# Recurrent branch of a hybrid encoder block: outputs of two row halves in one PSUM bank and one chain, the far score block issued with the step ahead of it, first scores one k tile later

## The chip, the cores and the metric

The kernel runs on one core of one Trainium2 chip. The time is device microseconds from launch to end, the median of several executions; the kernel before has 1391.43 us as the median of 3 runs (1390.93 to 1392.01). One more execution was profiled: it took 1390.61 us, of which the program's own instructions span 1388.9 us (1.7 us lie around them).

## The reference

One block over 256 rows of width 2048, in fp32: an RMSNorm, one wide projection, two branches side by side, a gated merge, an output projection, a second RMSNorm and a squared-ReLU MLP of width 8192, and a final norm. The change lies in the recurrent branch (HGRN2): 8 heads of 128 by 128, in chunks of 64 rows.

```python
f = sigmoid(hf); g = lb + (1 - lb) * f; log_g = log(g); kk = 1 - g
q = silu(hq) * 128 ** -0.5
# per head, chunk after chunk, b = cumsum(log_g) in the chunk:
o_inter = (q * exp(b)) @ S
scores  = sum_k q[t,k] * exp(b[t,k] - b[s,k]) * kk[s,k]     # s <= t
o       = o_inter + scores @ v
S       = exp(b_last)[:, None] * S + (kk * exp(b_last - b)).T @ v
y_a     = rms_norm(o, hg_norm_w) * silu(hg)
```

The other branch is chunked attention (16 heads of 64) with a relative bias, and comes behind the recurrent one in the kernel.

## The kernel before, in words

Every large product takes its operands as two fp32r parts, high and low. A weight tile of 128x1024 comes in by a DMA on SyncE's queue (`raw`), ScalarE (ACT) casts it into `wh` (line 91) and VectorE (DVE) subtracts to get `wl` (line 92); `wh` and `wl` have four buffers each, so the cast for a tile waits until TensorE (PE) has used up the tile four before it. `gemm_t` (lines 163 to 185) gives feature-major results, per k tile two matmuls of 512 columns with `wh` and two of 256 with `wl`; `gemm` (line 154) gives row-major ones, per k tile six matmuls of 512 columns. Both write `acc` tiles of two banks from the pool `ps_acc`, which has two buffers.

The recurrent branch has no stage of its own on PE. Its small fp32 matmuls are laid between the k tiles of the big products by a list of steps, `behind`: `later` appends steps with a number each, and `tick` (lines 144 to 149), called per k tile with 1 in `gemm_t` and 2 in `gemm`, counts the front step's number down and issues it when it reaches zero. Steps are issued in the order of the list. The scheduler then keeps the order of issue on each engine, except that what is issued at high priority (the weight splits, line 125; results, line 187; the last split of the outputs, line 491) goes ahead as soon as its inputs are expected.

The eight heads are four pairs (0 to 3). `scores` (line 515) appends for a pair the eight steps that `hgrn_scores` (line 357) returns at line 457: the first step (tiles `ps_10`, `ps_11`, one per head, then the factors of level 2), then factors and levels in turn. A level (line 406) multiplies for each head into a bank `ps` of pool `ps_sm` (tag "sm", two banks), and three predicated copies of DVE per head (line 421) merge it into the tile `sd` of a pair: `ps_20`, `ps_21` are level 2 of heads 0 and 1, likewise `ps_80` and `ps_320`. `level128` (line 442) makes the far block between the two row halves: two matmuls into `ps_128`, which ACT copies to `so`.

`hgrn_out` (line 461) makes the outputs of a pair. `outputs(m)` for row half m: `po` (`sd` times the values `v`, and for m = 1 also `so` times `v` of half 0) into a bank of `ps_sm`; ACT squares it (line 477), DVE sums the squares (478) and scales the sum (line 97), GpSimd (POOL) raises it to -0.5 (line 98), DVE multiplies `po` by that and the gate `gw` into `o` (483). `finish(m)` transposes the two heads' `o` into a bank `tpo` of pool `ps_tp` (tag "tp", two banks), and a split on ACT and DVE makes `act_ya`. `group` (line 533) appends the outputs of two pairs, and returns their finishing steps.

The calls at lines 545 to 561 set the order: the scores of pair 0 beside the products `hi` and `hg` of heads 0 to 3, those of pair 1 beside `hg`, `hf`, `hq`, the outputs of pairs 0 and 1 beside `hf` and `hq` of pair 3, and so on; the outputs of pairs 2 and 3 beside the products `aq`, behind which attention begins. A product is named by its column block in the traces: `acc_hi`, `acc_hq`, `acc_aq`, `acc_ak`. `aq0T` is the copy of the first `aq` product (lines 189 and 190).

Of the kernel before, what the change touches and what calls it, by code (L numbers as in the profile page):

```python
# [8 lines left out]
F32 = mybir.dt.float32  # L9
# [3 lines left out]
ALU = mybir.AluOpType  # L13
AX = mybir.AxisListType
PSUM = bass.MemoryType.PSUM

P = 128
T = 256
NM = T // P
# [7 lines left out]
DK = 128  # L27
# [23 lines left out]
def tile_hybrid_block(  # L51
# [5 lines left out]
    nc = tc.nc  # L57
# [14 lines left out]
    ident = const.tile([P, P], F32, name="ident")  # L72
# [17 lines left out]
    def split(hi, lo, src, copy=None):  # L90
        casts[:] = [(copy or nc.scalar.copy)(hi, src)]  # L91
        return nc.vector.tensor_tensor(lo, src, hi.bitcast(F32), op=ALU.subtract)  # L92

    def rsqrt(dst, ssq, n, width):

        ms = small.tile([P, width], F32, name="ms", tag=f"ms{width}")
        nc.vector.tensor_scalar(ms, ssq, 1.0 / n, EPS, op0=ALU.mult, op1=ALU.add)  # L97
        nc.gpsimd.tensor_tensor(dst, ms, mhalf[:, :width], op=ALU.pow)  # L98

# [51 lines left out]
    def later(*steps):  # L151
        behind.extend([n, f] for n, f in steps)
# [41 lines left out]
    hp = hpool_cm.__enter__()  # L194
# [164 lines left out]
    def hgrn_scores(n, made):  # L359

        kk, b, q = made["kk"], made["b"], made["q"]
        sd = hp.tile([P, 2, NM, P], F32, name=f"sd{n}", tag="sd", bufs=2)
        so = hp.tile([P, 2, P], F32, name=f"so{n}", tag="so", bufs=2)
# [77 lines left out]

        def level128():
            kc, ql = held["128"]
            ps = ps_sm.tile([P, 2, P], F32, name=f"ps{n}_128", tag="sm")
            for h in range(2):
                nc.tensor.matmul(ps[:, h, :], kc[:, h].rearrange("p v b -> p (v b)"),
                                 ql[:, h].rearrange("p v b -> p (v b)"), start=True, stop=True)
            nc.scalar.copy(so, ps)

        f = [lambda i=i, B=B: factors(i, B) for i, B in enumerate(LEVELS)]  # L450
        l = [lambda i=i, B=B: level(i, B) for i, B in enumerate(LEVELS)]
# [2 lines left out]
            diagonal()  # L454
            f[0]()

        return (sd, so), [first, f[1], l[0], f[2], l[1], factors128, l[2], level128]

    ya = []

    def hgrn_out(g, h0, sc, vs, gws):
        sd, so = sc
        n = f"{g}{h0}"
        hi, lo = ya[g][:, :, 0, :], ya[g][:, :, 1, :]
        os = []

        def outputs(m):
            po = ps_sm.tile([P, 2, DK], F32, name=f"po{n}{m}", tag="sm")
            for h in range(2):
                c = slice((h0 + h) * DK, (h0 + h + 1) * DK)  # L470
                if m:
                    nc.tensor.matmul(po[:, h, :], so[:, h, :], vs[0][:, c], start=True, stop=False)
                nc.tensor.matmul(po[:, h, :], sd[:, h, m, :], vs[m][:, c], start=m == 0, stop=True)
            o = hp.tile([P, 2, DK], F32, name=f"o{n}{m}", tag="o", bufs=4)
            sq = hp.tile([P, 2, DK], F32, name=f"osq{n}{m}", tag="osq", bufs=1)
            s2 = small.tile([P, 2], F32, name=f"os{n}{m}", tag="os")
            nc.scalar.activation(sq, po, AF.Square)
            nc.vector.tensor_reduce(s2, sq, axis=AX.X, op=ALU.add)
            ro = small.tile([P, 2], F32, name=f"ro{n}{m}", tag="ro")
            rsqrt(ro, s2, DK, 2)  # L480
            for h in range(2):
                c = slice((h0 + h) * DK, (h0 + h + 1) * DK)
                nc.vector.scalar_tensor_tensor(o[:, h, :], po[:, h, :], ro[:, h:h + 1], gws[m][:, c],
                                               op0=ALU.mult, op1=ALU.mult)
            os.append(o)

        def finish(m):
            tp = ps_tp.tile([P, 2, P], F32, name=f"tpo{n}{m}", tag="tp")
            for h in range(2):
                nc.tensor.transpose(tp[:, h, :], os[m][:, h, :], ident)  # L490
            with tc.high_priority(offset=2000):
                split(hi[:, h0:h0 + 2, m * P:(m + 1) * P], lo[:, h0:h0 + 2, m * P:(m + 1) * P], tp)

        return [lambda m=m: outputs(m) for m in range(NM)], [lambda m=m: finish(m) for m in range(NM)]

    def fq(u):
        if u == 0:
            f, z = f0, z0
        elif u == 1:
            f, z = f1, z1  # L500
        else:
            f, z = h2(f"f{u}"), h2(f"zq{u}")
            add_parts(f, gemm_t(xT, w_in_t, C_HF + u * T, KD, f"hf{u}"))
            add_parts(z, gemm_t(xT, w_in_t, C_HQ + u * T, KD, f"hq{u}"))
        made = {}

        def decay():
            made["g"], made["kk"], made["b"] = hf_pair(u, f)

        def query():  # L510
            made["q"] = hq_pair(u, z, made["g"])

        return made, decay, query

    def scores(n, made, gap, first=None, between=()):

        sc = []
        steps = []
# [8 lines left out]
        todo = [(gap if i or first is None else first, lambda i=i: one(i)) for i in range(8)]  # L527
        for at, f in between:
            todo.insert(at, (gap, f))
        later(*todo)  # L530
        return sc

    def group(g, s0, s1, vs, gws, gap, gap2):
        parts = {}

        def outputs(h0, sc, m):
            if not m:
                parts[h0] = hgrn_out(g, h0, sc, vs, gws)
            parts[h0][0][m]()

        later(*[(gap, lambda h0=h0, sc=sc, m=m: outputs(h0, sc, m)) for h0, sc in ((0, s0), (2, s1)) for m in range(NM)])
        return [(gap2, lambda h0=h0, m=m: parts[h0][1][m]()) for h0 in (0, 2) for m in range(NM)]
# [538 lines left out]
    for qd in range(NQ):  # L1081
# [70 lines left out]
        for n0 in (0, 2):  # L1152
# [3 lines left out]
                              start=0, tail=last and n0 == 2))  # L1156
# [47 lines left out]
```

## Time and profile before

| what | before |
|---|---|
| median of 3 runs | 1391.43 us |
| profiled execution | 1390.61 us |
| its span | 1388.9 us |
| PE busy | 1377.7 us, 99% |
| DVE busy | 1139.5 us, 82% |
| ACT busy | 925.6 us, 67% |
| POOL busy | 144.4 us, 10% |
| granted PE clock | 1.00 |
| recurrent steps on PE | 60.9 to 236 us |

A row of a group or of the timeline names the line, engine and operation, the tile written and the tiles read, and the shape; buffer numbers are left out. A small fp32 matmul stands as two records. A matmul's recorded length (0.39 us for 512 columns) overlaps the next one's; what it takes of PE is the distance from its start to the next start.

### The profile page before, as it was taken

Reading aid. Unit: us, or ns where it says so; the run is one execution under the profiler, and the core shown is the slowest. Engines: PE = TensorE matmul, PEld = TensorE weight load, DVE = VectorE, ACT = ScalarE, POOL = GpSimd, SP = SyncE. Lnnn points to the kernel's source line nnn. Section 1 sums busy time; section 2 is a strip of 40 time slices with the busy share of each in tenths; the row PEclk is TensorE's granted clock in tenths of the full one; section 3 lists DMA queues with packets and bytes.
Section 4 is the critical chain, followed back from the end, with each engine's and each line's share of the span. In section 5 each row is a group of like instructions: output and inputs, shape, how many; then the busy total and the mean of one; then the engine's idle time right before and its main releaser. Section 6 shows DMA issues by size and latency. Waiting matters only on the chain.

```text
span 1388.9 us, 18633 instructions
## 1 busy us (share of the span) xinstructions
PE 1377.7 (99%) x6550; PEld 1144.0 (82%) x6550; DVE 1139.5 (82%) x1429; ACT 925.6 (67%) x1193; POOL 144.4 (10%) x231
## 2 busy tenths in 40 slices
PE   9999999999999999999999999999999999999997
PEld 8889888878778888888888888888888888888886
DVE  7897997976878785697998977879877897878885
ACT  7774765665676664446777766678666876668864
POOL 2000001100100000001211001100011001110200
PEclk9999999999999999999999999999999999999999
DMA  9654445785679896558989789988899888998892
GB/s 339 226 175 158 153 166 178 224 280 167 161 213 279 265 268 222 191 171 272 287 224 309 246 257 299 259 255 252 249 291 301 249 236 251 277 299 260 259 283 100
DMA packets 124078, 331.62 MB, mean 239 GB/s; under 512 B 11072, under 2 KB 11840, under 8 KB 123600
## 3 DMA queue, kind: packets, MB, share of 16 engines
q1 hardware_dynamic: 103696, 265.59, 54.2%
q0 software_dynamic: 19568, 64.04, 23.5%
q8 instruction: 51, 0.84, 0.2%
q10 hardware_dynamic: 720, 0.81, 0.2%
q14 instruction: 43, 0.35, 0.1%
HBM read 271.67 MB, written 10.49 MB: 203 GB/s over the span
## 4 chain that ended last, share of the span: by engine, by line
PE 96%; DVE 2%; ACT 1%; issue 0%; DMA 0%; POOL 0%; SPq 0%; POOLq 0%; DVEq 0%; ACTq 0%
PE acc_ak L177 2%; PE acc_hf L177 2%; PE acc_aq L177 2%; PE acc_hq L177 2%; PE ps L414 1%; PE acc_ak L182 1%; PE tp_u L108 1%; PE acc_hg L136 1%; PE acc_hg L135 1%; PE acc_bb L135 1%; PE acc_bb L136 1%; PE acc_ba L135 1%; PE acc_ba L137 1%; PE acc_hg L137 1%; PE acc_ba L136 1%; PE acc_bb L137 1%
## 5 line engine op out<-in xcount | busy, mean ns | idle before, releaser
L177 PE MATMUL acc_aq<-act_x,wh_aq 128*128 128x512 f32 x128 | 42.4, 407 | 0.0
L177 PE MATMUL acc_hf<-act_x,wh_hf 128*128 128x512 f32 x128 | 41.4, 405 | 0.0
L177 PE MATMUL acc_hq<-act_x,wh_hq 128*128 128x512 f32 x128 | 40.7, 399 | 0.0
L177 PE MATMUL acc_ak<-act_x,wh_ak 128*128 128x512 f32 x128 | 40.1, 396 | 0.1
L91 ACT CAST wh_bb<-raw_bb 128x1024 fp32r<-128x1024 f32 x16 | 16.9, 1054 | 23.3 <-PE acc_ba L137 17.7
L91 ACT CAST wh_aq<-raw_aq 128x1024 fp32r<-128x1024 f32 x16 | 16.8, 1051 | 22.5 <-PE acc_hg L137 8.7
L92 DVE TENSOR_TENSOR wl_bb<-raw_bb,wh_bb 128x1024 fp32r<-128x1024 f32 x16 | 19.6, 1224 | 14.8 <-ACT wh_bb L91 14.8
L91 ACT CAST wh_ba<-raw_ba 128x1024 fp32r<-128x1024 f32 x16 | 16.8, 1053 | 21.0 <-PE acc_bb L137 13.8
L92 DVE TENSOR_TENSOR wl_ba<-raw_ba,wh_ba 128x1024 fp32r<-128x1024 f32 x16 | 19.6, 1224 | 12.6 <-ACT wh_ba L91 12.6
L92 DVE TENSOR_TENSOR wl_aq<-raw_aq,wh_aq 128x1024 fp32r<-128x1024 f32 x16 | 19.6, 1223 | 11.1 <-ACT wh_aq L91 11.1
L182 PEld LDWEIGHTS acc_hq<-act_x,wl_hq 128*128 128x128 f32 x128 | 23.4, 188 | 6.0 <-DVE wl_hq L92 0.8
L182 PEld LDWEIGHTS acc_ak<-act_x,wl_ak 128*128 128x128 f32 x128 | 23.5, 188 | 5.6 <-issue 0.3
L182 PEld LDWEIGHTS acc_hf<-act_x,wl_hf 128*128 128x128 f32 x128 | 23.6, 189 | 5.3
L182 PEld LDWEIGHTS acc_aq<-act_x,wl_aq 128*128 128x128 f32 x128 | 23.5, 189 | 4.8
L182 PE MATMUL acc_aq<-act_x,wl_aq 128*128 128x256 f32 x128 | 25.8, 285 | 0.0
L135 PE MATMUL acc_hi<-wh_hi,act_x 128*128 128x512 f32 x64 | 25.8, 403 | 0.0
L92 DVE TENSOR_TENSOR act_u<-tp_u,act_u 128x512 fp32r<-128x512 f32 x32 | 21.9, 686 | 4.7 <-ACT act_u L91 4.2
L98 POOL TENSOR_TENSOR ro<-ms,mhalf 128x2 f32<-128x2 f32 x8 | 5.9, 738 | 190.3 <-DVE ms L97 190.3
L135 PE MATMUL acc_hg<-wh_hg,act_x 128*128 128x512 f32 x64 | 25.7, 401 | 0.0
L135 PE MATMUL acc_bb<-wh_bb,act_yb 128*128 128x512 f32 x64 | 25.2, 393 | 0.0
L136 PE MATMUL acc_hi<-wl_hi,act_x 128*128 128x512 f32 x64 | 25.1, 392 | 0.0
L182 PE MATMUL acc_hq<-act_x,wl_hq 128*128 128x256 f32 x128 | 24.7, 279 | 0.4 <-DVE wl_hq L92 0.4
(1928 smaller groups left out, 5250.6 us busy)
## 6 DMA issues: line engine op xcount, KB each, us to landing
raw_hi<-in_w_in_n_dram SPq DMA_DIRECT2D x16, 512.0 KB, 4.1
raw_hg<-in_w_in_n_dram SPq DMA_DIRECT2D x16, 512.0 KB, 3.6
raw_aq<-in_w_in_t_dram SPq DMA_DIRECT2D x16, 512.0 KB, 3.9
raw_ak<-in_w_in_t_dram SPq DMA_DIRECT2D x16, 512.0 KB, 3.8
raw_ba<-in_w_branch_a_dram SPq DMA_DIRECT2D x16, 512.0 KB, 4.4
raw_bb<-in_w_branch_b_dram SPq DMA_DIRECT2D x16, 512.0 KB, 4.4
raw_hf<-in_w_in_t_dram SPq DMA_DIRECT2D x12, 512.0 KB, 3.6
raw_hq<-in_w_in_t_dram SPq DMA_DIRECT2D x12, 512.0 KB, 4.5
```

The costliest lines, as they stand in the source:

```text
L91: casts[:] = [(copy or nc.scalar.copy)(hi, src)]
L92: return nc.vector.tensor_tensor(lo, src, hi.bitcast(F32), op=ALU.subtract)
L98: nc.gpsimd.tensor_tensor(dst, ms, mhalf[:, :width], op=ALU.pow)
L108: nc.tensor.transpose(tp[:, j, :], src[:, j * P:(j + 1) * P], ident)
L135: nc.tensor.matmul(acc, hi, wh, start=first, stop=False, skip_group_check=True)
L136: nc.tensor.matmul(acc, hi, wl, start=False, stop=False, skip_group_check=True)
L137: nc.tensor.matmul(acc, lo, wh, start=False, stop=last, skip_group_check=True)
L177: nc.tensor.matmul(acc[:, cb, :], wh[:, cb * P:(cb + 1) * P], r.rearrange("p u t -> p (u t)"), start=kt == 0, stop=last)
L182: nc.tensor.matmul(acc[:, cb, 0:T], wl[:, cb * P:(cb + 1) * P], r[:, 0, :], start=False, stop=False)
L414: nc.tensor.matmul(ps[:, m, :], klf[:, a * P:(a + 1) * P], qrf[:, a * 192:(a + 1) * 192], start=True, stop=True)
```

## The change

Three things change.

1. `level128` is no longer a step of its own: it is issued right behind the last level, in one step, and its bank comes from `ps_tp` and no longer from `ps_sm`. A pair has 7 score steps and no longer 8.
2. `outputs` makes both row halves at once: one bank `po` of 128 x (2 x 2 x 128), one square, one sum, one scaling (in place), one power, and four products into one `o`. `finish` transposes all four blocks into one bank and makes one split of 128x512. The number of a step of outputs goes from 4 to 6 for pairs 0 and 1 and from 2 to 3 for pairs 2 and 3, that of a finishing step from 3 and 2 to 6.
3. The number of pair 0's first step goes from 13 to 15, which is one k tile of `gemm`.

```diff
-    def rsqrt(dst, ssq, n, width):
+    def rsqrt(dst, ssq, n, width, ms=None):
-        ms = small.tile([P, width], F32, name="ms", tag=f"ms{width}")
+        if ms is None:
+            ms = small.tile([P, width], F32, name="ms", tag=f"ms{width}")
...
         def level128():
-            ps = ps_sm.tile([P, 2, P], F32, name=f"ps{n}_128", tag="sm")
+            ps = ps_tp.tile([P, 2, P], F32, name=f"ps{n}_128", tag="tp")
...
-        return (sd, so), [first, f[1], l[0], f[2], l[1], factors128, l[2], level128]
+        def final():
+            l[2]()
+            level128()
+        return (sd, so), [first, f[1], l[0], f[2], l[1], factors128, final]
...
-        def outputs(m):
-            po = ps_sm.tile([P, 2, DK], F32, name=f"po{n}{m}", tag="sm")
+        def outputs():
+            po = ps_sm.tile([P, NM, 2, DK], F32, name=f"po{n}", tag="sm")
+            for m in range(NM):
+                for h in range(2):
+                    c = slice((h0 + h) * DK, (h0 + h + 1) * DK)
+                    if m:
+                        nc.tensor.matmul(po[:, m, h, :], so[:, h, :], vs[0][:, c], start=True, stop=False)
+                    nc.tensor.matmul(po[:, m, h, :], sd[:, h, m, :], vs[m][:, c], start=m == 0, stop=True)
...
+            nc.vector.tensor_reduce(s2, sq.rearrange("p m h d -> p (m h) d"), axis=AX.X, op=ALU.add)
+            rsqrt(ro, s2, DK, NM * 2, s2)
...
-        def finish(m):
-            tp = ps_tp.tile([P, 2, P], F32, name=f"tpo{n}{m}", tag="tp")
+        def finish():
+            tp = ps_tp.tile([P, 2, T], F32, name=f"tpo{n}", tag="tp")
+            for m in range(NM):
+                for h in range(2):
+                    nc.tensor.transpose(tp[:, h, m * P:(m + 1) * P], os[0][:, m, h, :], ident)
...
-    s0 = scores(0, a0[0], 5, 13, ((5, a1[1]), (8, a1[2])))
+    s0 = scores(0, a0[0], 5, 15, ((5, a1[1]), (8, a1[2])))
-    turns0 = group(0, s0, s1, vs0, gws0, 4, 3)
+    turns0 = group(0, s0, s1, vs0, gws0, 6, 6)
-    later(*group(1, s2, s3, vs1, gws1, 2, 2))
+    later(*group(1, s2, s3, vs1, gws1, 3, 6))
```

The program's order shows three places. The first is PE at pair 0's first scores, beside the product `hi`. Before, `ps_10` stood ahead of the first matmul of k tile 6 and `ps_11` one matmul later:

```order
L137 MATMUL acc_hi_650<-wh_hi_4_688,act_x_108 128x512
L370 MATMUL ps_10_713<-q_646,kk_636 128x192 x2
L135 MATMUL acc_hi_650<-wh_hi_6_706,act_x_108 128x512
L370 MATMUL ps_11_718<-q_646,kk_636 128x192 x2
L136 MATMUL acc_hi_650<-wl_hi_6_707,act_x_108 128x512
L137 MATMUL acc_hi_650<-wh_hi_6_706,act_x_108 128x512
```

After the change both stand together behind the six matmuls of that k tile (line numbers of the change are one higher here):

```order
L138 MATMUL acc_hi_650<-wh_hi_6_706,act_x_108 128x512
L136 MATMUL acc_hi_650<-wh_hi_6_706,act_x_108 128x512
L137 MATMUL acc_hi_650<-wl_hi_6_707,act_x_108 128x512
L138 MATMUL acc_hi_650<-wh_hi_6_706,act_x_108 128x512
L371 MATMUL ps_10_719<-q_646,kk_636 128x192 x2
L371 MATMUL ps_11_724<-q_646,kk_636 128x192 x2
L136 MATMUL acc_hi_650<-wh_hi_6_706,act_x_108 128x512
```

So `ps_10` moved back by six matmuls of 512 columns and `ps_11` by five.

The second place is DVE at the outputs of pairs 0 and 1. Before, the sum (478), its scaling (97) and the products that wait for POOL (483) stood right behind one another, with a weight split between two such chains:

```order
L478 TENSOR_REDUCE os_1416<-osq_1415 128x2
L97 TENSOR_SCALAR ms<-os_1416 128x2
L483 SCALAR_TENSOR_TENSOR o_1414<-po_1411,ro_1419,gw_1067 128x128 x2
L92 TENSOR_TENSOR wl_hq_4_1550<-raw_hq_4_1548,wh_hq_4_1549 128x1024
L478 TENSOR_REDUCE os_1454<-osq_1453 128x2
L97 TENSOR_SCALAR ms<-os_1454 128x2
L483 SCALAR_TENSOR_TENSOR o_1452<-po_1447,ro_1457,gw_1071 128x128 x2
```

Now the chain of pair 0 stands among the factors of pair 2 (`b`, `el_2`, `er_2`, `q`):

```order
L322 SCALAR_TENSOR_TENSOR b_1480<-reset,lg_1478 128x512
L484 TENSOR_REDUCE os_1394<-osq_1393 128x4
L382 TENSOR_TENSOR el_2_1624<-b_1480 128x512
L98 TENSOR_SCALAR os_1394<-os_1394 128x4
L387 TENSOR_TENSOR er_2_1627<-b_1480 128x64x6
L490 SCALAR_TENSOR_TENSOR o_1392<-po_1385,ro_1397,gw_1071 128x128 x2
L490 SCALAR_TENSOR_TENSOR o_1392<-po_1385,ro_1397,gw_1075 128x128 x2
L92 TENSOR_TENSOR wl_hq_0_1524<-raw_hq_0_1522,wh_hq_0_1523 128x1024
L333 SCALAR_TENSOR_TENSOR q_1503<-zq_1080,sq_1501 128x4x128
```

Pair 2's work on DVE moved ahead of the outputs, and one chain stands where two were.

The third place is PE at the first scores of pair 2. Before, they stood behind k tile 2 of the second `hi` product:

```order
L135 MATMUL acc_hi_1644<-wh_hi_2_1669,act_x_107 128x512
L136 MATMUL acc_hi_1644<-wl_hi_2_1670,act_x_107 128x512
L137 MATMUL acc_hi_1644<-wh_hi_2_1669,act_x_107 128x512
L370 MATMUL ps_10_1699<-q_1590,kk_1562 128x192 x2
L370 MATMUL ps_11_1704<-q_1590,kk_1562 128x192 x2
```

Now they stand in the last quarter of the product ahead of it, `hq` of pair 3:

```order
L178 MATMUL acc_hq_1521<-act_x_109,wh_hq_8_1574 128x512 x2
L183 MATMUL acc_hq_1521<-act_x_109,wl_hq_8_1575 128x256 x2
L178 MATMUL acc_hq_1521<-act_x_110,wh_hq_12_1603 128x512 x2
L183 MATMUL acc_hq_1521<-act_x_110,wl_hq_12_1604 128x256 x2
L371 MATMUL ps_10_1614<-q_1503,kk_1475 128x192 x2
L371 MATMUL ps_11_1619<-q_1503,kk_1475 128x192 x2
```

Between the two positions lie the last three k tiles of `hq` (six matmuls of 512 columns, six of 256) and the first four of `hi` (24 of 512 columns): that far did the scores of pair 2 move forward. Pair 1's first scores moved forward in the same way by four k tiles of `gemm_t`, and each later level with them.

More of the change, by code (lines that the diff above doesn't have):

```diff
@@ L487, in finish @@
[L487 to L490 removed]
+        def outputs():
[6 more added lines that the diff above has]
+                    nc.tensor.matmul(po[:, m, h, :], sd[:, h, m, :], vs[m][:, c], start=m == 0, stop=True)
+            o = hp.tile([P, NM, 2, DK], F32, name=f"o{n}", tag="o", bufs=2)
+            sq = hp.tile([P, NM, 2, DK], F32, name=f"osq{n}", tag="osq", bufs=1)
+            s2 = small.tile([P, NM * 2], F32, name=f"os{n}", tag="os")
+            nc.scalar.activation(sq, po, AF.Square)
+            nc.vector.tensor_reduce(s2, sq.rearrange("p m h d -> p (m h) d"), axis=AX.X, op=ALU.add)
+            ro = small.tile([P, NM * 2], F32, name=f"ro{n}", tag="ro")
+            rsqrt(ro, s2, DK, NM * 2, s2)
+            for m in range(NM):
+                for h in range(2):
+                    c = slice((h0 + h) * DK, (h0 + h + 1) * DK)
+                    nc.vector.scalar_tensor_tensor(o[:, m, h, :], po[:, m, h, :], ro[:, 2 * m + h:2 * m + h + 1], gws[m][:, c],
+                                                   op0=ALU.mult, op1=ALU.mult)
+            os.append(o)
@@ L491, in finish @@
+        def finish():
+            tp = ps_tp.tile([P, 2, T], F32, name=f"tpo{n}", tag="tp")
+            for m in range(NM):
+                for h in range(2):
+                    nc.tensor.transpose(tp[:, h, m * P:(m + 1) * P], os[0][:, m, h, :], ident)
             with tc.high_priority(offset=2000):
-                split(hi[:, h0:h0 + 2, m * P:(m + 1) * P], lo[:, h0:h0 + 2, m * P:(m + 1) * P], tp)
-        return [lambda m=m: outputs(m) for m in range(NM)], [lambda m=m: finish(m) for m in range(NM)]
+                split(hi[:, h0:h0 + 2, :], lo[:, h0:h0 + 2, :], tp)
@@ L496, in fq @@
+        return outputs, finish
     def fq(u):
@@ L525, in one @@
             steps[i]()
-        todo = [(gap if i or first is None else first, lambda i=i: one(i)) for i in range(8)]
+        todo = [(gap if i or first is None else first, lambda i=i: one(i)) for i in range(7)]
         for at, f in between:
@@ L534, in group, with outputs @@
         parts = {}
[L536 to L542, printed above, removed]
+        def outputs(h0, sc):
+            parts[h0] = hgrn_out(g, h0, sc, vs, gws)
+            parts[h0][0]()
+        later(*[(gap, lambda h0=h0, sc=sc: outputs(h0, sc)) for h0, sc in ((0, s0), (2, s1))])
+        return [(gap2, lambda h0=h0: parts[h0][1]()) for h0 in (0, 2)]
     ya += [new_act(f"ya{g}") for g in range(2)]
```

15 lines of the change are left out of this document (removed).

## The prediction

> **What bounds the kernel now.** I read the page's busy times first, then busy time by stretches.
>
> ```profile
> span 1388.9 us, 18633 instructions
> PE 1377.7 (99%) x6550; PEld 1144.0 (82%) x6550; DVE 1139.5 (82%) x1429; ACT 925.6 (67%) x1193; POOL 144.4 (10%) x231
> ...
> 60.00:100.00 40.00, 39.72 (x183) 33.16 (x182) 39.37 (x91) 28.80 (x40) 0.00 (x0) 1.00 0.50 172
> 130.00:160.00 30.00, 29.93 (x180) 26.15 (x179) 24.34 (x46) 22.41 (x31) 3.15 (x4) 1.00 0.45 153
> 160.00:190.00 30.00, 30.00 (x145) 25.72 (x144) 30.00 (x74) 21.27 (x31) 0.00 (x0) 1.00 0.45 153
> 400.00:1380.00 980.00, 980.00 (x4421) 810.97 (x4421) 804.29 (x780) 669.29 (x805) 108.75 (x136) 1.00 0.85 253
> ```
>
> PE bounds it everywhere: from 400 us on it is busy in all of 980 us, at full clock, and the recurrent steps (61 to 236 us) run beside it. The change leaves PE the same matmuls, so it can win only time that PE loses waiting. Recorded busy time hides most of that, since a matmul's recorded length overlaps the next one; I measure it from start to start. DVE is the second engine: 24.34 of 30 us busy beside the outputs of pairs 0 and 1, but all 30.00 of 30 beside the scores of pair 2, and 39.37 of 40 beside those of pair 0.
>
> **Fewer, larger groups on PE: nothing.** The change merges 12 groups of small matmuls into others (4 far blocks, 4 outputs, 4 transposes). Does leaving the large product and coming back cost something?
>
> ```profile
> 70.97 1.46 PE L414 MATMUL ps<-qr,kl 128*128 128x192 f32 x8
> 72.13 0.53 PE L135 MATMUL acc_hi<-wh_hi,act_x 128*128 128x512 f32 x1
> 72.50 0.40 PE L136 MATMUL acc_hi<-wl_hi,act_x 128*128 128x512 f32 x1
> ```
>
> Eight records of 0.33 us ending 1.46 us after their first start are (1.46 - 0.33) / 7 = 0.161 apart. A 512-column matmul takes 0.227 (rows 60.20 and 60.42 below stand 0.22 apart, and longer undisturbed stretches give 0.227). From 70.97 to 72.50 are 1.53 us; 8 x 0.161 + 0.227 = 1.52. The 0.37 us behind the group only pays back its last record's early handover. The upper bound would be that 0.14 us each, 12 x 0.14 = 1.7 us; the sum above excludes nearly all of it, and I take 0.
>
> **First scores one k tile later: gain 0.8 us.**
>
> ```profile
> 60.20 0.39 PE L136 MATMUL acc_hi<-wl_hi,act_x 128*128 128x512 f32 x1
> 60.42 0.39 PE L137 MATMUL acc_hi<-wh_hi,act_x 128*128 128x512 f32 x1
> 60.90 0.92 PE L370 MATMUL ps<-q,kk 128*128 128x192 f32 x4
> 61.52 0.53 PE L135 MATMUL acc_hi<-wh_hi,act_x 128*128 128x512 f32 x1
> 62.24 0.92 PE L370 MATMUL ps<-q,kk 128*128 128x192 f32 x4 [0.18 <-DVE q L335]
> 62.86 0.52 PE L136 MATMUL acc_hi<-wl_hi,act_x 128*128 128x512 f32 x1
> 63.22 0.39 PE L137 MATMUL acc_hi<-wh_hi,act_x 128*128 128x512 f32 x1
> ...
> 60.56 0.28 DVE L335 TENSOR_TENSOR q<-q,f 128x128 f32<-128x128 f32 x1
> 61.90 0.29 DVE L335 TENSOR_TENSOR q<-q,f 128x128 f32<-128x128 f32 x1
> ```
>
> From 60.42 to 63.22 are 2.80 us, with work for 3 x 0.227 + 8 x 0.161 = 1.97: PE lost 0.83 us waiting for `q` of each head, the second written at 62.19. Six large matmuls later PE comes to `ps_10` at 60.42 + 7 x 0.227 = 62.01 and to `ps_11` at 62.66, behind both. What is late next: `ps_20` then also comes 1.36 - 0.83 = 0.5 us later than now, and DVE has its factors ready before that; cost 0, and if that cover went, at most the 0.5 us.
>
> **Waits for a bank: gains 0.28, 0.55 and 0.37 us.**
>
> ```profile
> 155.45 0.62 PE L177 MATMUL acc_hq<-act_x,wh_hq 128*128 128x512 f32 x2
> 156.14 0.44 PE L490 MATMUL tpo<-ident,o 128*128 128x128 f32 x2
> 156.34 0.48 PE L135 MATMUL acc_hi<-wh_hi,act_x 128*128 128x512 f32 x1
> 156.65 0.40 PE L136 MATMUL acc_hi<-wl_hi,act_x 128*128 128x512 f32 x1
> ...
> 155.66 0.43 DVE L92 TENSOR_TENSOR act_ya<-tpo,act_ya 128x256 fp32r<-128x256 f32 x1
> ...
> 227.82 0.39 PE L182 MATMUL acc_aq<-act_x,wl_aq 128*128 128x256 f32 x2
> 228.53 0.46 PE L472 MATMUL po<-v,so 128*128 128x128 f32 x2 [0.32 <-DVE o L483]
> 228.82 0.39 PE L473 MATMUL po<-v,sd 128*128 128x128 f32 x2
> ...
> 227.77 0.61 DVE L483 SCALAR_TENSOR_TENSOR o<-po,ro,gw 128x128 f32<-128x128 f32 x2 [0.87 <-POOL ro L98]
> ...
> 237.59 0.63 PE L177 MATMUL acc_aq<-act_x,wh_aq 128*128 128x512 f32 x2
> 238.30 0.73 PE L177 MATMUL acc_ak<-act_x,wh_ak 128*128 128x512 f32 x2
> 238.87 0.28 PE L182 MATMUL acc_ak<-act_x,wl_ak 128*128 128x256 f32 x1
> ...
> 236.16 0.37 ACT L91 CAST act_ya<-tpo 128x256 fp32r<-128x256 f32 x1
> 236.42 0.59 ACT L189 COPY aq0T<-acc_aq 128x512 f32<-128x512 f32 x1
> 237.57 0.68 DVE L190 TENSOR_TENSOR aq0T<-acc_aq,aq0T 128x512 f32<-128x512 f32 x1
> ```
>
> The third transpose waits until DVE has emptied the first one's bank (155.66 + 0.43 = 156.09): 155.45 to 156.65 is 1.20 us for three large matmuls and two records of about 0.12, that is 0.92; lost 0.28. The fourth `po` waits for the bank that `o` frees at 228.38: 0.48 us before it (two 256-column matmuls at 0.116) and 0.07 within, 0.55. The first `acc_ak` waits for the bank of the first `aq` product, which ACT copies only behind the last `act_ya` cast (236.16) and DVE adds until 238.25: 237.59 to 238.87 is 1.28 us for four matmuls, 0.91; lost 0.37. With one `po` and one `tpo` per pair, two banks serve two pairs without reuse; in the order the last transposes now stand behind the first k tile of the second `aq` product, fifteen k tiles (15 x 2 x (0.227 + 0.116) = 10.3 us) ahead of the first `acc_ak`, and `aq0T` can follow about 2 us behind them. All three waits go. Together with the first scores: 0.83 + 0.28 + 0.55 + 0.37 = 2.0 us.
>
> **What the chains cost now: 0.4 us.** A chain now is square, sum, scaling, power, four products. DVE pays POOL's latency four times, not eight:
>
> ```profile
> 223.59 0.17 DVE L97 TENSOR_SCALAR ms<-os 128x2 f32<-128x2 f32 x1
> 223.91 0.69 POOL L98 TENSOR_TENSOR ro<-ms,mhalf 128x2 f32<-128x2 f32 x1 [71.24 <-DVE ms L97]
> 224.63 0.35 DVE L483 SCALAR_TENSOR_TENSOR o<-po,ro,gw 128x128 f32<-128x128 f32 x1 [0.87 <-POOL ro L98]
> ...
> L1131 POOL TENSOR_TENSOR rstd<-rstd,mhalf x2: 553/566/578, 1377.1 to 1382.3; 128x1 f32<-128x1 f32 x2
> ```
>
> A power takes 0.57 us for one column and 0.69 for two; four are by that line 0.69 + 2 x 0.12 = 0.94 (bounds 0.69 and 1.38). The products then start 1.04 + 0.25 = 1.3 us behind the scaling. Queued behind them on DVE stand weight splits of 1.23 us, which PE needs 4 to 5 us later; they cover it.
>
> ```profile
> 235.00 1.05 ACT L91 CAST wh_ak<-raw_ak 128x1024 fp32r<-128x1024 f32 x1
> ...
> 236.09 1.23 DVE L92 TENSOR_TENSOR wl_ak<-raw_ak,wh_ak 128x1024 fp32r<-128x1024 f32 x1 [0.43 <-ACT wh_ak L91]
> ```
>
> The tight place is the last pair's transpose: in the order its fourth product stands behind `wl_aq_8`, whose cast can start only when PE frees a buffer, five k tiles (5 x 0.69 = 3.4 us) ahead of that transpose; cast 1.05, split 1.23 and product 0.35 are 2.63 before any handover or any other work of DVE. So 0 to 1.2 us (one split more in front) for this pair, the same at most for the others; I take 0.4 for all, near the lower end because the three others have 2 us to spare.
>
> [...]
>
> **Score banks: 0.3 us.** The scores of pair 2 come to PE six 512-column matmuls, six of 256 (0.116) and 24 of 512 earlier, 30 x 0.227 + 6 x 0.116 = 7.5 us. They use the two banks that `po` held, and each next level waits for DVE's copies out of the last one. That work leaves the full stretch (30.00 of 30) for the one with 5.7 us free, and DVE itself saves up to four POOL waits of 0.87, 3.5 us. Where a weight split stands before the copies, they are late by 1.23 us. Bounds 0 and four levels x 1.23 = 4.9; no `ps` wait of this kind shows even in the full stretch, so I take 0.3.
>
> **Attention's start: 0, bounds -0.9 and +0.9 us.** Its first scores move five k tiles ahead of their place, because `aq0T` is early. PE loses 0.9 us in the 150 us behind its start:
>
> ```profile
> 250.00:400.00 150.00, 149.08 (x801) 117.67 (x800) 121.31 (x208) 96.41 (x168) 16.03 (x34) 1.00 0.69 205
> ```
>
> It can go or double.
>
> **Sum.** -2.0 + 0.4 + 0.3 + 0 = -1.3 us. The profiled execution took 1390.6 us, 1388.9 of span and 1.7 around it; it becomes 1389.3. The median of the runs is 0.8 us above the profiled one: 1391.4 - 1.3 = **1390.1 us**, 0.1% faster.
>
> **Rivals.**
> - *More comes back* (12%): no chain is late, the score banks cost nothing, and attention's 0.9 us go too: -2.9 us, 1388.5, just over 0.2%. For it speaks DVE's saving; against it that some of attention's waits are for ACT's own copies, which the change leaves.
> - *Attention takes it back* (12%): its first scores, now ahead of DVE's last weight splits, wait 0.7 us more at two places: -1.3 + 1.4 us, about 1391.5, no change.
> - *Score banks bind* (14%), slower: pair 2's levels each wait for copies behind a split, four times 1.23 us, 4.9 - 2.0 + 0.4 = +3.3, 1394.7. It decides from the point where DVE comes more than about 1 us behind its present distance to PE at pair 2's second level; a POOL power near 1.4 us twice in front of that would do half of it. The 30.00 of 30 us speak for it, the 5.7 us free before against it.
> - *The change does not do what it says*: the order shows the moves, and the banks' owners are fixed by the tiles; no chance of its own.
>
> **How the numbers follow.** My forecast, -2.0 to -0.3 us, has 62%. Faster by over 0.2% (2.8 us, about what a measurement of this kernel can tell from no change) is the first rival, 12%; slower by over 0.2% the third, 14%; within is the forecast and the second rival, 74%. The range runs from 1388.4 to 1393.4: the first rival's price less the runs' scatter of 0.5 below it would be 1388.0, which I cut a little; above it takes in half of the third rival.
>
> **What would show it.** Right: from 60 to 250 us no gap at `q`, `tpo`, `po` and `acc_ak`; the `hi` and `hq` products of pair 2 start at the times above less 0.8 to 1.5 us; attention's first scores about 6 us earlier; nothing else moves behind 400 us but by a constant of 1 to 2 us. Wrong: PE rows of `ps` with DVE `sd` as releaser between 150 and 176 us; a POOL power over 1.2 us; `tpo` waiting for `o` by more than 0.5 us; or a loss from 250 to 320 us above 1 us.

## The result, and the profile after

The changed kernel takes 1389.14 us (median of 21 runs, 1388.22 to 1390.24) against 1391.62 us for the kernel before (21 runs): 2.5 us less, a ratio of 0.9984 with a 95% interval of 0.9978 to 0.9990, which is 1.4 to 3.1 us. The forecast was 1.3 us less. Four executions of the whole study, which took 300 us more or longer, are left out of all medians and intervals. The profiled execution took 1389.94 us, above its own median, while that of before lay below its own, so the two spans differ by only 0.8 us. To compare the kernels themselves I take two matmuls that both have: the last of k tile 5 of the product `hi` (in the prediction's row 60.42 for before) and the first `wh_ga0r` matmul behind a `pa`, near 390 us. In every kernel of this study the second is the 1777th record behind the first. I call the time between them the **distance**. It is read from one profiled execution of each kernel. How well it repeats shows in its last 700 records, in attention: they take 131.25 to 131.50 us in the eleven kernels that have them in the order of the changed kernel, and 131.19 to 131.27 us in the three that have them in the order of before. A difference of 0.3 us says little by itself. First two rows of the page after, then the matmul starts that bound the distance, of after:

```profile
span 1388.1 us, 18593 instructions
...
PE 1376.7 (99%) x6550; PEld 1143.5 (82%) x6550; DVE 1137.7 (82%) x1417; ACT 922.7 (66%) x1185; POOL 143.4 (10%) x227
```

```profile
60.72 0.39 PE L138 MATMUL acc_hi<-wh_hi,act_x 128*128 128x512 f32 x1
...
390.94 0.50 PE L136 MATMUL acc_ga0c<-wh_ga0r,act_x 128*128 128x512 f32 x1
```

and the second of them before:

```profile
393.11 0.50 PE L135 MATMUL acc_ga0c<-wh_ga0r,act_x 128*128 128x512 f32 x1
```

Before it is 393.11 - 60.42 = 332.69 us, after 390.94 - 60.72 = 330.22: 2.47 us less, the difference of the medians. The rest of the two spans (0.3 us more ahead of 60 us, 1.4 us more behind 393) is scatter of single executions: over the fourteen profiles the first of the two matmuls starts at 60.4 to 61.9 us, and the last matmul ends 987.8 to 989.2 us behind the second. Busy time by stretches after, with the columns as in the prediction's table (the stretch and its length; busy us and number of instructions of PE, PE's weight loads, DVE, ACT and POOL; granted clock, DMA share, GB/s):

```profile
60.00:100.00 40.00, 40.00 (x189) 34.03 (x188) 39.49 (x90) 29.13 (x41) 0.00 (x0) 1.00 0.53 182
130.00:160.00 30.00, 30.00 (x182) 26.71 (x181) 27.33 (x53) 24.00 (x33) 2.38 (x2) 1.00 0.45 147
160.00:190.00 30.00, 30.00 (x145) 25.78 (x144) 29.93 (x73) 19.50 (x27) 0.00 (x0) 1.00 0.48 159
...
400.00:1380.00 980.00, 979.72 (x4418) 809.70 (x4416) 802.41 (x779) 668.41 (x805) 108.80 (x136) 1.00 0.85 253
```

PE is now busy in all of the first three. DVE is fuller between 130 and 160 us (27.33 for 24.34), as the prediction said, and PE loses nothing by it. From start to start, against the usual length of each form of matmul, PE lost 3.5 us from 60 to 240 us before and 1.4 us after; from 240 to 400 us, where attention runs, 10.6 and 10.2.

The first scores, PE and then DVE:

```profile
62.08 0.39 PE L138 MATMUL acc_hi<-wh_hi,act_x 128*128 128x512 f32 x1
62.30 1.46 PE L371 MATMUL ps<-q,kk 128*128 128x192 f32 x8
63.47 0.53 PE L136 MATMUL acc_hi<-wh_hi,act_x 128*128 128x512 f32 x1
63.83 0.40 PE L137 MATMUL acc_hi<-wl_hi,act_x 128*128 128x512 f32 x1
...
60.85 0.28 DVE L336 TENSOR_TENSOR q<-q,f 128x128 f32<-128x128 f32 x1
...
62.18 0.28 DVE L336 TENSOR_TENSOR q<-q,f 128x128 f32<-128x128 f32 x1
```

All eight records run together now; the second `q` ends at 62.46, ahead of `ps_11`, whose turn comes at 62.30 + 4 x 0.163 = 62.95. The three waits for banks are gone too: the transposes of pair 1 (150.52 us) and the outputs of pair 3 (215.58 us) each start 0.23 us behind the start of the two 256-column matmuls ahead of them, which is what those take. The last transposes and the first `acc_ak` on PE, and what stands around them on ACT and DVE:

```profile
225.73 0.60 PE L498 MATMUL tpo<-ident,o 128*128 128x128 f32 x4
...
236.16 0.63 PE L178 MATMUL acc_aq<-act_x,wh_aq 128*128 128x512 f32 x2
236.63 0.62 PE L178 MATMUL acc_ak<-act_x,wh_ak 128*128 128x512 f32 x2
...
226.36 0.59 ACT L91 CAST act_ya<-tpo 128x512 fp32r<-128x512 f32 x1
226.84 0.59 ACT L190 COPY aq0T<-acc_aq 128x512 f32<-128x512 f32 x1
...
225.57 0.34 DVE L490 SCALAR_TENSOR_TENSOR o<-po,ro,gw 128x128 f32<-128x128 f32 x1
...
228.06 0.68 DVE L191 TENSOR_TENSOR aq0T<-acc_aq,aq0T 128x512 f32<-128x512 f32 x1
```

The bank behind `aq0T` is free when DVE's addition ends, at 228.74 us, 7.9 us before PE wants it at 236.63 (before, the bank came 0.4 us too late).

### The profile page after: what moved, and what is told of

The parts are those of the page before. It is cut to its first block, busy times and chain, and to the rows that moved or that the text cites. A ratio compares the mean times of both kernels' runs of the same rounds, so it can differ in the third digit from the quotient of the medians.

```text
span 1388.1 us, 18593 instructions
## 1 busy us (share of the span) xinstructions
PE 1376.7 (99%) x6550; PEld 1143.5 (82%) x6550; DVE 1137.7 (82%) x1417; ACT 922.7 (66%) x1185; POOL 143.4 (10%) x227
## 4 chain that ended last, share of the span: by engine, by line
PE 89%; DMA 5%; DVE 3%; issue 2%; ACT 1%; POOL 0%; POOLq 0%; SPq 0%; ACTq 0%; DVEq 0%
PE acc_ak L178 2%; PE acc_aq L178 2%; PE acc_hf L178 2%; PE acc_hq L178 2%; PE ps L415 1%; PE acc_ak L183 1%; PE acc_hg L137 1%; PE acc_hi L137 1%; PE acc_bb L136 1%; PE acc_hi L138 1%; PE acc_hg L136 1%; PE acc_bb L137 1%; PE acc_ba L136 1%; PE acc_hi L136 1%; PE acc_ba L138 1%
## 5 line engine op out<-in xcount | busy, mean ns | idle before, releaser
L92 DVE TENSOR_TENSOR wl_hf<-raw_hf,wh_hf 128x1024 fp32r<-128x1024 f32 (+2 forms) x21 | 20.5, 976 | 6.1 <-ACT wh_hf L91 5.7
L91 ACT CAST wh_ak<-raw_ak 128x1024 fp32r<-128x1024 f32 x16 | 16.8, 1051 | 12.9 <-PE acc_aq L178 5.5
```

## The experiments

Theory A: PE loses time only where a wait ends last on it, so what counts is at which time each step comes to PE against its tiles and banks; a part of the change has no value of its own. Rivals: each part brings its own saving (B), or merging itself saves, by fewer groups on PE and fewer chains (C); D, E and F are named where an experiment tests them. Each experiment has 8 to 11 runs beside the kernel before. Its profile gives the distance; the two columns agree within 0.6 us. Where they differ I go by the distance, which contains nothing but the stretch in question, though it is one execution's.

| run | what it has | distance minus that of before, us | median minus that of before, us | ratio of times, 95% interval |
|---|---|---|---|---|
| changed kernel | 1, 2, 3 | -2.47 | -2.5 | 0.9978 to 0.9990 |
| e1_first15 | 3 | +4.02 | +3.6 | 1.0019 to 1.0040 |
| e2_after13 | 1, 2 | -1.67 | -1.8 | 0.9979 to 0.9996 |
| e3_far_only | 1 | +2.36 | +2.4 | 1.0010 to 1.0028 |
| e4_outputs_only | 2 | -0.72 | -0.1 | 0.9989 to 1.0007 |
| e10_far_first15 | 1, 3 | -0.22 | -0.1 | 0.9989 to 1.0007 |
| e11_outputs_first15 | 2, 3 | -0.33 | -0.2 | 0.9990 to 1.0007 |
| e5_far_sm | far block in a score bank | +0.14 | +0.4 | 0.9996 to 1.0014 |
| e12_far_own_step | far block its own step | -1.55 | -1.0 | 0.9984 to 1.0002 |
| e6_half_chains | chain per half | +3.45 | +3.0 | 1.0012 to 1.0030 |
| e9_one_square | one square, then per half | -2.45 | -2.2 | 0.9978 to 0.9995 |
| e8_short_gaps | finishing steps at 3 | +1.33 | +1.7 | 1.0002 to 1.0020 |
| e7_halves_room | halves apart, new numbers | -1.19 | -1.2 | 0.9983 to 1.0001 |

### Each part alone, and two together

**e1_first15**, on the kernel before:

```diff
-    s0 = scores(0, a0[0], 5, 13, ((5, a1[1]), (8, a1[2])))
+    s0 = scores(0, a0[0], 5, 15, ((5, a1[1]), (8, a1[2])))
```

> Only the first scores of the kernel before move one k tile later (13 becomes 15); outputs, banks and far blocks stay. Theory A (PE loses time only at waits; what counts is which wait ends last): the 0.83 us at ps_10 and ps_11 go, but all recurrent steps behind them come 1.4 to 2.7 us later on PE, the last transposes by about 2 us, and the copy aq0T, which stands behind the last act_ya cast on ACT, with them; the first acc_ak then waits about 2.3 us in place of 0.37. Attention gives back some 0.4 us. Sum -0.83 + 1.9 - 0.4 = +0.7 us, between -0.2 and +1.5; PE's distance from 60 to 390 us longer by that. Theory B (each part brings its own saving, independent of the others): -0.83 us.

Slower by 3.6 us; B falls. The waits that end on PE (the bracket gives its idle time and what ended it), and the clock (the first of the last three numbers) around the longest:

```profile
189.88 0.57 PE L446 MATMUL ps<-ql,kc 128*128 128x128 f32 x3 [1.27 <-DVE sd L421]
...
241.47 0.73 PE L177 MATMUL acc_ak<-act_x,wh_ak 128*128 128x512 f32 x2 [2.04 <-DVE aq0T L190]
```

```profile
241.40:242.80 1.40, 1.33 (x7) 1.14 (x8) 1.40 (x3) 0.00 (x0) 0.15 (x1) 0.97 0.86 228
242.80:246.00 3.20, 3.20 (x12) 2.81 (x11) 2.76 (x5) 0.44 (x1) 0.00 (x0) 0.50 1.00 390
246.00:248.00 2.00, 2.00 (x12) 1.70 (x12) 1.36 (x2) 1.13 (x2) 0.00 (x0) 0.97 0.99 367
```

The wait at the first `acc_ak` is the one A asked for (2.2 us from start to start, 2.3 expected). Two things were not: the far block of pair 2 waits 1.43 us for a score bank that DVE empties behind a weight split, and after the 2.04 us of idle PE's granted clock fell to 0.50 for 3.4 us (242.7 to 246.1, worked out from the three rows), which costs 1.6 us more.

**e2_after13**, the changed kernel with 15 back to 13:

> The changed kernel with the first scores back at 13. Theory A: the two waits of 0.83 us for q come back between 60 and 64 us, everything behind keeps its distances, since the last transposes come 1.4 us earlier still and no wait stands behind them: 0.83 us slower than the changed kernel, 1.6 us faster than the kernel before (local distance from 60 to 390 us 2.48 - 0.83 = 1.65 us shorter than before). Theory B gives the same here.

As expected: 0.80 us more than the changed kernel in distance. In the company of the other parts the later first scores are worth their 0.8 us, alone they cost 4.

**e3_far_only** (on the kernel before, `group` and `outputs` untouched):

```diff
-            ps = ps_sm.tile([P, 2, P], F32, name=f"ps{n}_128", tag="sm")
+            ps = ps_tp.tile([P, 2, P], F32, name=f"ps{n}_128", tag="tp")
...
-        return (sd, so), [first, f[1], l[0], f[2], l[1], factors128, l[2], level128]
+        return (sd, so), [first, f[1], l[0], f[2], l[1], factors128, final]
...
-        todo = [(gap if i or first is None else first, lambda i=i: one(i)) for i in range(8)]
+        todo = [(gap if i or first is None else first, lambda i=i: one(i)) for i in range(7)]
```

> Only part 1 on the kernel before: the far block is issued with the last level, in a bank of the transposes, and the pair has seven score steps; outputs stay in halves. Theory A: the score steps and outputs of pairs 2 and 3 come 6 to 11 us earlier on PE, the last transposes end near 225 us, aq0T follows, and the waits for po, tpo and acc_ak (0.55, 0.28 and 0.37 us) go although nothing is merged; attention gives about 0.4 us; the 0.83 us of the first scores stay: -1.6 us, between -0.8 and -2.0. Theory C (the merging itself is what saves: fewer groups on PE at 0.14 us each, fewer POOL waits): four groups fewer, -0.56 us, and the po and tpo waits stay.

My number failed: 2.4 us slower. `acc_ak` no longer waits, as said, but the chains, whose outputs and transposes come to PE 4 to 10 us earlier, are not ready:

```profile
140.22 0.46 PE L476 MATMUL po<-v,so 128*128 128x128 f32 x2 [1.46 <-DVE o L487]
...
227.29 0.33 PE L494 MATMUL tpo<-ident,o 128*128 128x128 f32 x1 [0.31 <-DVE o L487]
...
229.93 0.30 PE L494 MATMUL tpo<-ident,o 128*128 128x128 f32 x1 [0.67 <-DVE o L487]
```

**e4_outputs_only** (the changed kernel with the lines of e3 and the 15 taken back):

> Only part 2: both halves' outputs in one bank and chain with the new step numbers; the far block stays a step of its own, the first scores stay at 13. Theory A: the po and tpo waits (0.55 and 0.28 us) go, the last transposes come to PE at about 232.5 us, still 4 us ahead of the first acc_ak, so its wait shrinks from 0.37 to 0 to 0.3 us, attention gives 0.4: -1.3 us, between -0.8 and -1.7. Theory C: eight groups fewer at 0.14 us, -1.1 us, spread over all groups and not at the waits.

The distance is 0.72 us shorter, just under the expected 0.8 to 1.7: the waits of `po`, `tpo` and `acc_ak` are gone, 1.2 us, and attention gains 0.2, but pair 2's far block waits 0.46 us for its score bank, and smaller gaps take 0.2. The median's interval holds no change.

**e10_far_first15** (e3 with 15) and **e11_outputs_first15** (the changed kernel with e3's lines taken back):

> Parts 1 and 3 on the kernel before, without part 2 (halves stay apart, with the old step numbers). Theory A: the first scores' 0.83 us go, and since the last transposes stand at 225 us, far ahead of aq0T, nothing turns on them; the po wait of 1.6 us and the tpo waits of 1.7 us of the run with part 1 alone stay: +2.4 - 0.8 = 1.6 us slower than the kernel before. If each part brought its own saving: -0.83 + 2.4, the same here.

> Parts 2 and 3 on the kernel before, without part 1 (the far block is a step of its own in a score bank). Theory A: the first scores' 0.83 us go; steps of pairs 2 and 3 come 8 us later than in the changed kernel, with the last transposes at 234 us, so aq0T makes the first acc_ak wait by 0 to 0.6 us; the far block of pair 2 or 3 waits 0.5 to 1.4 us for a score bank: 1.0 us faster than the kernel before, between 0.2 and 1.8. Adding the parts' own results (-0.1 and +3.6) would give 3.5 us slower.

e10 came out 1.8 us better than expected in distance: its `tpo` waits stay (0.38, 0.47 and 0.85 us), but `po` waits no more: DVE frees its bank at 139.31 us for 140.07 in e3, and PE comes to it at 139.79. Counted from the last matmul of k tile 5, which is 0.6 us later in e10's profile, DVE is 1.4 us sooner and PE 0.6 us later. e11 is at the weak end of its bounds, with the two waits that A named: 1.04 us for the score bank and 0.39 us at the first `acc_ak`.

```profile
185.00 0.68 PE L447 MATMUL ps<-ql,kc 128*128 128x128 f32 x4 [0.88 <-DVE sd L422]
```

The three parts alone sum to 4.02 + 2.36 - 0.72 = 5.7 us slower; together they are 2.5 us faster. Part 3 needs the earlier end that part 1 gives (beside part 2 alone, e11 against e4, it costs 0.4 us), part 1 needs the fewer chains of part 2 (or numbers that give eight chains room, see e7), and part 2 needs part 1's bank.

### The far block: its bank or its step?

**e5_far_sm**, the changed kernel with

```diff
-            ps = ps_tp.tile([P, 2, P], F32, name=f"ps{n}_128", tag="tp")
+            ps = ps_sm.tile([P, 2, P], F32, name=f"ps{n}_128", tag="sm")
```

> The changed kernel with the far block's bank taken from the score banks again; it stays in one step with the last level. Theory A (the far block must not need a score bank, because DVE copies those out behind weight splits): the last level takes both score banks just ahead, so ps_128 waits for DVE's sd copies of head 0, 0.3 to 1.4 us at each of four pairs, as the far block did by 1.43 us for pair 2 when only the first scores were moved: 1.5 us slower than the changed kernel, between 0.5 and 4. Theory D (the bank does not matter, the saved step does): no difference, within 0.3 us.

2.6 us slower than the changed kernel in distance (0.14 + 2.47), within A's bounds, though in one place and not in four:

```profile
178.23 0.68 PE L447 MATMUL ps<-ql,kc 128*128 128x128 f32 x4 [1.89 <-DVE sd L422]
...
175.86 1.22 DVE L92 TENSOR_TENSOR wl_hi<-raw_hi,wh_hi 128x1024 fp32r<-128x1024 f32 x1
176.99 1.30 DVE L422 COPY_PREDICATED sd<-masks,ps 128x192 f32<-128x192 int32 x5
```

The weight split stands ahead of the copies on DVE. In the changed kernel the same DVE work lies at the same place, and PE does not wait for it:

```profile
173.39 1.46 PE L415 MATMUL ps<-qr,kl 128*128 128x192 f32 x8
174.69 0.61 PE L447 MATMUL ps<-ql,kc 128*128 128x128 f32 x4
175.05 0.48 PE L136 MATMUL acc_hi<-wh_hi,act_x 128*128 128x512 f32 x1
...
175.51 1.22 DVE L92 TENSOR_TENSOR wl_hi<-raw_hi,wh_hi 128x1024 fp32r<-128x1024 f32 x1
176.65 1.31 DVE L422 COPY_PREDICATED sd<-masks,ps 128x192 f32<-128x192 int32 x5
```

**e12_far_own_step**, the changed kernel with `final` taken back to two steps (and 8 for 7), the bank left:

> The changed kernel with the far block as a step of its own again, but left in a transpose bank: part 1 without its saved step. Theory A (of part 1 the bank is what PE's time needs; the saved step only brings the last transposes forward, which counts for aq0T alone): no wait at ps_128; last transposes at 234 us, first acc_ak waits 0 to 0.5 us: 0.3 us slower than the changed kernel, between 0 and 0.8. Theory F (the step ahead is what helps): the run differs from the changed kernel as the one with parts 2 and 3 does, by over 1 us.

No `ps_128` waits; the first `acc_ak` waits 0.39 us. In distance it is 0.9 us slower than the changed kernel, a little over A's bound of 0.8 and just short of the 1 us that F asks for; the other half is lost in attention, at a copy that the changed kernel no longer waits for (it comes up again below):

```profile
269.14 0.50 PE L136 MATMUL acc_avc<-wh_avp12C,S_x 128*128 128x512 f32 x1 [0.37 <-ACT acc_avc L755]
```

So the bank keeps PE from the wait, and the step brings the end of the recurrent branch forward. Both count: of the 2.1 us that separate e11, which lacks the whole of part 1, from the changed kernel, e12 wins back 1.2 by the bank alone, and the step is worth the other 0.9.

### The chains

**e6_half_chains** makes square, sum, scaling, power and products per half, in the shared bank:

```diff
-            nc.scalar.activation(sq, po, AF.Square)
-            nc.vector.tensor_reduce(s2, sq.rearrange("p m h d -> p (m h) d"), axis=AX.X, op=ALU.add)
...
-            rsqrt(ro, s2, DK, NM * 2, s2)
             for m in range(NM):
+                c2 = slice(2 * m, 2 * m + 2)
+                nc.scalar.activation(sq[:, m], po[:, m], AF.Square)
+                nc.vector.tensor_reduce(s2[:, c2], sq[:, m], axis=AX.X, op=ALU.add)
+                rsqrt(ro[:, c2], s2[:, c2], DK, 2, s2[:, c2])
...
```

> The changed kernel with the chain (square, sum, scaling, power, products) made for each half apart, but still one bank, one transposing step and one act_ya split of a pair. Theory A (one chain per pair is needed since POOL's latency stands on it twice otherwise): the last o of pairs 2 and 3 is ready with 0.4 and about 0 us to spare now and comes about 1 us later, so tpo waits for o, 0.5 to 1.5 us in all. Theory D (chains have cover): 0, within 0.3 us. If the square of half 0 starts before PE has written half 1, one bank does not hold ACT back; if it starts behind it, the bank or the tile does.

5.9 us slower than the changed kernel, four times A's upper bound. The square of pair 0's half 1 on ACT, `tpo` of pair 1 on PE, and the stretch behind it:

```profile
137.98 0.39 ACT L486 ACTIVATE osq<-po 128x256 f32<-128x256 f32 x1 [0.79 <-DVE o L491]
...
153.32 0.58 PE L499 MATMUL tpo<-ident,o 128*128 128x128 f32 x2 [2.00 <-DVE o L491]
```

```profile
154.60:158.00 3.40, 3.40 (x14) 2.93 (x13) 2.78 (x5) 0.91 (x1) 0.00 (x0) 0.57 0.49 188
```

ACT's square of half 1 waits for DVE's products of half 0, which end at 137.34 + 0.61 = 137.95 us: the two chains stand end to end. PE's waits at `tpo` are 2.2, 0.7 and 1.1 us, and behind the first the granted clock is low again (0.57 from 154.6 to 158.0 us), which costs 1.5 us more. **e9_one_square** has one square again and leaves the rest per half; against e6:

```diff
+            nc.scalar.activation(sq, po, AF.Square)
...
             for m in range(NM):
                 c2 = slice(2 * m, 2 * m + 2)
-                nc.scalar.activation(sq[:, m], po[:, m], AF.Square)
```

> As the run with a chain for each half in one bank, but with one square for the whole pair, so that ACT reads the bank once, ahead of DVE; sum, scaling, power and products stay in halves. Theory A now: that run lost 5.8 us because ACT's square of half 1 waited for DVE's products of half 0 in the same bank, which put the two chains end to end; with one square only POOL's second power and the second sum and scaling are left, 1.1 us more on a chain, against 2.5, 0.4 and 0 us to spare at pairs 1, 2 and 3: 1.4 us slower than the changed kernel, between 0.5 and 2.5. Theory E (POOL's second power was the cost, not the bank): 4 to 6 us slower, as in that run.

Like the changed kernel to 0.02 us in distance. E falls: POOL's second power costs nothing; what cost was that ACT and DVE read `po` in turns. Whether that order follows the bank or the tile in it no run separates. A's 1.4 us are wrong too; pair 2's chain shows why:

```profile
216.61 0.16 DVE L98 TENSOR_SCALAR os<-os 128x2 f32<-128x2 f32 x1
...
218.74 0.60 DVE L491 SCALAR_TENSOR_TENSOR o<-po,ro,gw 128x128 f32<-128x128 f32 x2
219.26 0.16 DVE L98 TENSOR_SCALAR os<-os 128x2 f32<-128x2 f32 x1
...
220.22 0.61 DVE L491 SCALAR_TENSOR_TENSOR o<-po,ro,gw 128x128 f32<-128x128 f32 x2 [0.49 <-POOL ro L99]
```

The first half's power lies beside other DVE work, and the last product ends at 220.83. In the changed kernel the one chain of pair 2 (DVE and POOL) ends at 219.59 + 1.13 = 220.72, which is no sooner, since k tile 5 ends 0.3 us earlier in that profile:

```profile
218.31 0.16 DVE L98 TENSOR_SCALAR os<-os 128x4 f32<-128x4 f32 x1
...
218.55 1.01 POOL L99 TENSOR_TENSOR ro<-os,mhalf 128x4 f32<-128x4 f32 x1 [72.27 <-DVE os L98]
...
219.59 1.13 DVE L490 SCALAR_TENSOR_TENSOR o<-po,ro,gw 128x128 f32<-128x128 f32 x4 [0.53 <-POOL ro L99]
...
221.10 0.60 PE L498 MATMUL tpo<-ident,o 128*128 128x128 f32 x4
```

**e8_short_gaps**, the changed kernel with `group(0, ..., 6, 3)` and `group(1, ..., 3, 3)`:

> The changed kernel with the number of a finishing step 3 in place of 6, for all pairs; nothing else. Theory A (a chain now takes 8 to 10 us from the last po to the last o, and the step number must cover it): transposes come to PE 2 to 4 us earlier than now, before o is ready: tpo waits for o about 0.6 us at pair 1 and 1.2 us at pairs 2 and 3 together, 1.8 us slower than the changed kernel, between 0.5 and 3. Theory D (chains have cover, nothing waits): 0, within 0.3 us.

3.8 us slower than the changed kernel, over A's bound of 3; D falls. `tpo` waits at pair 1 (0.40 and 1.27 us), 2 and 3 (0.54 and 1.11). At pair 1 a weight split of 1.22 us stands on DVE ahead of the fourth product, which I had not counted:

```profile
149.83 0.33 PE L498 MATMUL tpo<-ident,o 128*128 128x128 f32 x1 [1.10 <-DVE o L490]
...
148.29 1.22 DVE L92 TENSOR_TENSOR wl_hq<-raw_hq,wh_hq 128x1024 fp32r<-128x1024 f32 x1
149.43 0.35 DVE L490 SCALAR_TENSOR_TENSOR o<-po,ro,gw 128x128 f32<-128x128 f32 x1
```

**e7_halves_room**, e3 with 15 and `group(0, ..., 5, 2)`, `group(1, ..., 3, 3)`:

> Halves stay apart (eight banks, chains and transposes as before), with the far block joined to the last level in a transpose bank, first scores at 15, and new numbers that give the chains room: outputs 5 and transposes 2 for pairs 0 and 1, 3 and 3 for pairs 2 and 3. The last transpose then stands at 229 us on PE, ahead of what aq0T needs. Theory A (placement is all; merging only buys room): waits at po and tpo under 0.5 us each, 1.5 to 2.5 us faster than the kernel before, like the changed kernel. Theory C (eight chains and two banks cannot keep pace, merging is needed): po and tpo waits of 3 us stay as in the run with the far block alone, less the 0.83 of the first scores: 1.5 us slower than the kernel before.

1.19 us less than before in distance, short of A's 1.5 to 2.5 and far from C's 1.5 more. One `po` still waits for its bank (0.46 us), the rest is four smaller gaps of 0.1 to 0.2 us. With other numbers alone, eight chains in halves reach half of the gain. Whether better numbers would reach all of it stays open.

## Why the prediction was right, and where its terms were off

Point by point, against the working on record:

- *Fewer, larger groups: 0.* Right. From start to start the joined far block takes 1.755 us, its parts took 1.308 + 0.447; the joined outputs 1.341 to 1.352 for 0.447 + 0.894; four transposes 0.448 to 0.458 for two times 0.232. C's saving by fewer groups falls with it; fewer chains alone saved nothing either (e9).
- *First scores: 0.83.* Right in size (e2 against the changed kernel: 0.80), with a condition that the prediction did not see: e1 shows that without the earlier end of the branch the same step costs 4 us. The prediction put "what is late next" at `ps_20`; in e1 it is the far block of pair 2, about 125 us later, and the last transposes with `aq0T` behind them, over 170 us later.
- *Waits for a bank: 1.2.* Right: from 60 to 240 us PE lost 2.04 us less, the sum of these and the first scores.
- *Chains: 0.4.* Too much: 0. The last pair's fourth product, on which the term rested, ends at 225.91, and the transposes that start at 225.73 need it only as their last. But the cover is thin: three k tiles less and e8 loses 3.8 us. One of the prediction's signs of being wrong, a POOL power over 1.2 us, did appear (1.26 us, pair 0) and cost nothing, because that pair's transposes come 8 us behind it.
- *Score banks: 0.3, third rival 3.3 us slower.* 0. The prediction priced the levels' waits for copies behind a weight split; that wait exists (1.43 us in e1, 0.46 in e4, 1.04 in e11, 2.06 in e5), but it meets the far block, one more user of the same two banks, which the change takes out of them. I had read that move in the diff and given it no price.
- *Attention: 0, bounds -0.9 and +0.9.* -0.4. What went is one wait for ACT's copy of an `acc_avc` bank, before:

```profile
268.30 0.49 PE L135 MATMUL acc_avc<-wh_avp11D,act_x 128*128 128x512 f32 x1
269.16 0.50 PE L135 MATMUL acc_avc<-wh_avp12C,S_x 128*128 128x512 f32 x1 [0.37 <-ACT acc_avc L752]
```

and after:

```profile
266.55 0.50 PE L136 MATMUL acc_avc<-wh_avp11D,act_x 128*128 128x512 f32 x1
266.88 0.60 PE L618 MATMUL tpp<-ident,sb 128*128 128x128 f32 x4
267.35 0.50 PE L136 MATMUL acc_avc<-wh_avp12C,S_x 128*128 128x512 f32 x1
```

The first scores of attention come 5.6 us earlier (6 were forecast), and its first transposes `tpp` now stand in this gap of 0.64 us; 0.1 us is lost elsewhere. The order decides it, not how late the branch ends: e11 and e12, in which the last 700 records stand in the order of before, have the wait again (0.63 us each), and the other experiments, which have the changed kernel's order there, do not, e4 included, whose branch ends as late as e12's. The prediction called these copies something "which the change leaves": the copy stays, the idle time beside it does not.

So the step that gained was right, -2.0 us. The mis-sized terms are the two that took back (0.7 forecast, 0 measured) and attention (-0.4): -2.4, as the distance says. The measured 2.5 us lie outside the forecast's own range of 0.3 to 2.0 and nearer to the first rival (2.9), which had 12%; they lie inside the full range, which also holds no change and a slower kernel and so says little. What was right is the cause, the four waits; that what they gave was not taken back was foreseen only as a rival. The third rival's mechanism is real and was one bank away: e5, the change with that bank left where it was, comes out no faster than the kernel before.

That ACT comes behind PE's records of both halves in the shared bank cost PE nothing in the changed kernel: the one square of a pair, which reads both, began 0.03 to 2.1 us behind the end of the pair's last `po` record (pair 3 at 217.11 us, behind 216.69 + 0.39 = 217.08; pair 1 at 139.79, behind 137.28 + 0.39 = 137.67), and no `tpo` waited for the chain. What bound in e6 was ACT behind DVE: the square of half 1 began at 137.98, behind the products of half 0, which ended at 137.95. Whether ACT must also wait for PE's writing of the other half no run shows: in e6 the square of pair 0's half 0 begins at 133.95 us, behind PE's last record of that pair (132.17 + 0.39 = 132.56), but also straight behind ACT's own earlier work.

## What to carry to other kernels

When an engine is full and only a few waits are left, an edit to the order of work is worth what the next wait behind it allows: follow each moved step to the last thing that waits for it, even where that is another stage, and do not add the values of parts measured alone. Where two users share few banks, ask which of them is emptied by an engine whose queue holds long work; that user wants the other pool. In a shared bank the reads of two engines stood one behind the other here (e6: DVE's to 137.95 us, ACT's from 137.98), so read it once for the whole, and split behind that if need be (e9).

## What the runs showed of the hardware

- In two runs a wait cost nearly twice its length. After 2.04 us (e1) and 2.00 us (e6) without a matmul the granted clock fell: in e1 it was 0.50 from 242.8 to 246.0 us, in e6 0.82 from 153.3 to 154.6 and 0.57 from 154.6 to 158.0, and at its lowest a k tile took 1.28 us from start to start in both, for 0.70 otherwise. With 0.50 as the low clock these means give about 3.4 us of it in each run, an estimate; it cost 1.6 and 1.5 us more. After 1.89 us (e5) and 1.46 us (e3) the clock stayed at 1.00 (from 178.2 to 185.0 us and from 140.2 to 145.0). Why 2.00 us without a matmul lowered it and 1.89 us did not no run shows.
- POOL's power of four columns took 1.01 to 1.26 us in the changed kernel (mean of the group row 1.10; one of 1.98 us in e2, at no cost), for 0.94 estimated from one and two columns:

```profile
L99 POOL TENSOR_TENSOR ro<-os,mhalf 128x4 f32<-128x4 f32 x4 | 4.4, 1098 | 180.9 <-DVE os L98 180.9
```
